# RWKV main part of a one-layer decoder trunk: packed operands, fewer transposes, a written order on four engines, and one filling block moved forward

## The chip, the cores and the metric

The kernel runs on one core of one Trainium2 chip. The core has five engines that run their own instruction streams in order: PE (matrix products and transposes, from a weight load and a moving operand), DVE (vector work), ACT (activations and copies), POOL (general vector work, and the issue of some DMAs) and SP (which here only issues DMAs). An instruction waits for semaphores that other engines or DMAs raise. The metric is the device time in microseconds of one execution: before, a median of 1507.03 us of 3 runs (1506.78 to 1507.43).

## What is computed

One layer of a hybrid decoder trunk, sequence 1024, model width 1024. Its mixing stage projects the normed input to 30 blocks of 128 columns and feeds three groups of heads:

```python
z = rmsnorm(h, norm_mix_g[l]) @ w_in[l]
a_q, a_f, a_i, a_g, b_q, b_k, b_v, c_in = jnp.split(z, splits, axis=-1)
o_a = hgrn2_mix(a_q, a_f, a_i, a_g, ...)          # 4 heads
o_b = dilated_window_mix(b_q, b_k, b_v)           # 4 heads, three dilations
o_c, v_first = rwkv7_mix(c_in, ...)               # 4 heads of 64
h = h + jnp.concatenate([o_a, o_b, o_c], axis=-1) @ w_out[l]
```

A gated convolutional feed-forward part and a gated per-layer embedding follow. The change is in `rwkv7_mix`, whose core is a recurrence over the sequence, one state matrix of 64 x 64 per head:

```python
def step(state, inp):
    r_t, w_t, k_t, v_t, kk_t, a_t = inp
    sa = jnp.einsum('bhvk,bhk->bhv', state, -kk_t)
    state = (state * w_t[:, :, None, :] + sa[..., None] * (kk_t * a_t)[:, :, None, :]
             + v_t[..., None] * k_t[:, :, None, :])
    return state, jnp.einsum('bhvk,bhk->bhv', state, r_t)
```

and whose result is normed per head (mean and variance over 64 values), gets a bonus term and a gate.

## The kernel before

**Projections.** One block of 128 output columns over the whole sequence is 8 K tiles times 2 halves of 512 columns, each as three products of split operands (high by high, low by high, high by low: L127, L129, L131), so 48 matmuls of 128x512. Input and weight are each split into a high and a low part (`xh`, `xl`, `whi`, `wlo`); the weight's low part is made on POOL or DVE in turn (`split_w`). `project_rest` makes such a block, finishes it (scaling on DVE, for some kinds a sigmoid on ACT, into `zst`, L440 to L447) and stores it by SP to a DRAM tile (L437), from which the HGRN and window stages load it later (`zload`, L475, into `zl`). These blocks are the filling: their products need nothing of RWKV's work.

**RWKV.** The four heads go in two pairs, one head on each half of the 128 partitions. For each pair `rwkv_prep` makes the decayed keys and the rest, `rwkv_inverse` inverts the triangular systems inside the chunks (`T` and `U` quads), then filling blocks follow, then `rwkv_main`, then more filling. The list `FILL = (6, 4, 4, 4)` says how many blocks are taken: one of the first six inside the preparation of pair one and five behind it, four around and behind its main part, one and three ahead of pair two's main part, four behind. The remaining four blocks of 22 are made in the HGRN stage by `project_late` (L449), in eight halves, tile name `zp`.

**The main part.** The sequence is 16 chunks of 64; `rwkv_group` does four chunks (u = 0 to 3) at a time, so four groups per pair. In a group:

- the removal keys (first half of `ar`), the keys `be` (bhat) and `kh` (khat) are copied into block-diagonal tiles `abd`, `bbd`, `kbd` (one 64x64 block per head), and each of the four chunks of each is transposed on PE (`pt`, L758, 4 transposes each); `v` is transposed directly (L762, 2 transposes). ACT copies the results to `xr`, `rb`, `kt`, `vt`
- `py` (L789, T by the spread scores AB), `sc` (L794, keys by `ar`), `pu` (L799, Y by U), `pk` (L804) build the operands
- `px` (L810) is U against `xr`, 192 columns a chunk: 128 of the block-diagonal removal keys, 64 values. `pgm` (L817) is X against `rb`, 256 columns a chunk: 128 for the output, 128 for the state, both block-diagonal, and DVE adds a block-diagonal `addend` (L818, GM)
- `pn` (L822, L823) is the state's own term; the state runs through the four chunks (`pS`, L836, then DVE, L837), and the output `pyo` takes three products a chunk (L838, L839, L841). ACT copies it to `y`, a tile of its own.

After the third group and after the third following block, `rwkv_norm` norms a half of `y`, transposes it (`yt`) and applies bonus and gate (`oc`).

**What sets the order.** A scheduler orders each engine's instructions by priorities and modelled times, except inside a `manual_schedule` block, where the engines named keep the order in which the code is written. In RWKV, before, only the preparation on PE stands in such a block; the main part is left to the scheduler, which puts single dense matmuls of the next filling block between the small ones and pulls one block of filling ahead of pair two's main part.

**The HGRN stage.** Two chains of HGRN heads (tiles `hsc`, `hpo`, `hk`, `qt`, `ho`), the window attention (`swq`, `swt`, `swo`) and the late halves F are interleaved by a written list (L322 to L325): at each odd round below 16 stands one F. A pair of HGRN heads ends with the normed output: sums `hss` on DVE, `hrs` on POOL (L998), `ho` on DVE (L1000), its transposes `vt` on PE (L1006) and a last DVE step into `zl` (L1007). The second pair of window heads is loaded by two DMAs that POOL issues (L475).

Of the kernel before, what the change touches and what calls it, by code (L numbers as in the profile page):

```python
# [10 lines left out]
F32 = mybir.dt.float32  # L11
# [3 lines left out]
ALU = mybir.AluOpType  # L15
# [3 lines left out]
P = 128  # L19
# [60 lines left out]
class Trunk:  # L80
# [11 lines left out]
    def load_w(self, src):  # L92
        nc = self.nc
        raw = self.wpool.tile([P, 1024], F32, tag="wraw", name=self.nm("wraw"), bufs=2)
        nc.sync.dma_start(raw, src)
        return self.split_w(raw)
# [12 lines left out]
    def split_w(self, raw):  # L109

        parts = []
        for b in (0, 1):
            self.uid += 1
            parts.append(self.split2(raw[:, b * HT:(b + 1) * HT], self.nc.gpsimd if self.uid % 2 else self.nc.vector))
# [190 lines left out]
    def phase_mix(self):  # L305
# [8 lines left out]
        with tc.tile_pool(name="hg", bufs=1) as slots, tc.tile_pool(name="sw", bufs=1) as sp:  # L314
# [8 lines left out]
            for r in range(36):  # L323
                order += "C" * (r in self.TURNS) + "A" + "B" * (r > 5) + "F" * (r % 2 and r < 16)
# [98 lines left out]
    def project_rest(self, js, hooks={}):  # L423


        nc = self.nc
        for j in js:
            ps = self.proj(j, hooks)
            t = self.keep.tile([P, T], F32, tag="zst", name=self.nm("zst"), bufs=2)
            kind = (j - 8) % 4 if j < 24 else 2  # L430
            parts = [(t, ps, self.R)]
            if j < 24 and kind < 3:
                parts = [(t[:, :HT], ps[:, HT:][:, ::-1], self.R[:, HT:][:, ::-1]), (t[:, HT:], ps[:, :HT], self.R[:, :HT])]
            for part in parts:
                self.finish(kind, *part)
            d = self.zpool.tile([P, T], F32, tag=f"z{j}", name=f"z{j}")
            nc.sync.dma_start(d, t)  # L437
            self.z[j] = d
# [50 lines left out]
    def rwkv(self):  # L489
# [7 lines left out]
        for p in (0, 1):  # L497
# [5 lines left out]
            self.project_rest([next(js) for _ in range(self.FILL[2 * p] - 1)])  # L503
            with tc.tile_pool(name=f"rk{p}", bufs=1) as rp:
                self.rwkv_main(p, rp, sg, d)
            for i in range(self.FILL[2 * p + 1]):
                self.project_rest([next(js)])
                if i == 2:
                    self.rwkv_norm(p, sg, d, 1)
        self.rest = list(js)  # L510

    FILL = (6, 4, 4, 4)

    def rwkv_prep(self, p, tp, lt, d, j):
# [51 lines left out]
        ar = self.slots.tile([P, 16, 2, 64], F32, tag="rk_ar", name=self.nm("ar"), bufs=1)  # L566
# [57 lines left out]
    def scores_open(self, d):  # L624
        for n in ("sc", "rb"):
            d[n] = self.slot(n).rearrange("p (c i) -> p c i", i=64)
# [47 lines left out]
    def rwkv_main(self, p, rp, sg, d):  # L674
        y = self.slot("y")
        y3 = y.rearrange("p (c v) -> p c v", v=64)
        S = None
        d.update(y=y, y3=y3)
        for g in range(4):
            S = self.rwkv_group(p, g, rp, d, y3, S)  # L680
            if g == 2:
                self.rwkv_norm(p, sg, d, 0)

    def rwkv_norm(self, p, sg, d, hf):

        nc, mxp, par = self.nc, self.mxp, self.par
        y, y3 = d["y"], d["y3"]
# [4 lines left out]
        sl, cs = slice(hf * HT, (hf + 1) * HT), slice(8 * hf, 8 * hf + 8)  # L692
        y, y3 = y[:, sl], y3[:, cs, :]
        if hf == 0:
            d["o"] = self.keep.tile([P, T], F32, tag="oc", name=self.nm("oc"), bufs=2)
        o = d["o"][:, sl]
        mean = self.spool.tile([P, 8], F32, tag="kr1", name=self.nm("gnm"), bufs=1)
        nc.vector.tensor_reduce(mean, y3, AX.X, ALU.add)
        nc.vector.tensor_scalar(mean, mean, 1.0 / 64, None, ALU.mult)
        nc.vector.tensor_tensor(y3, y3, mean.unsqueeze(2).broadcast_to([P, 8, 64]), ALU.subtract)  # L700
        nc.scalar.activation(o, y, AF.Square)
        var = self.spool.tile([P, 8], F32, tag="kr2", name=self.nm("gnv"), bufs=1)
        nc.vector.tensor_reduce(var, o.rearrange("p (c v) -> p c v", v=64), AX.X, ALU.add)
        nc.vector.tensor_scalar(var, var, 1.0 / 64, GN_EPS, ALU.mult, ALU.add)
        rs = self.spool.tile([P, 8], F32, tag="kr3", name=self.nm("gnr"), bufs=1)
        nc.gpsimd.tensor_tensor(rs, var, self.mhalf[:, :8], ALU.pow)
        nc.vector.tensor_tensor(y3, y3, rs.unsqueeze(2).broadcast_to([P, 8, 64]), ALU.mult)
# [16 lines left out]
    def rwkv_group(self, p, g, rp, d, y3, S):  # L724

        nc, mxp = self.nc, self.mxp
        cs = slice(4 * g, 4 * g + 4)
        ar, v, gC = d["ar"], d["v"], d["gC"]

        def c3(t):  # L730
            return t.rearrange("p (c i) -> p c i", i=64)[:, cs, :]
# [3 lines left out]

        ab = self.block_diag(rp, "abd", ar[:, cs, 0, :], nc.scalar)
        bb = self.block_diag(rp, "bbd", c3(d["be"]), nc.gpsimd)
        kb = self.block_diag(rp, "kbd", c3(d["kh"]), nc.gpsimd)
        if (rp, "add") not in self.bd:
            add = rt("addend", [P, 4, 2, 2, 64])  # L740
            nc.gpsimd.memset(add, 0.0)
            for u in range(4):
# [1010 lines left out]
```

## Time and profile before

| what | value |
|---|---|
| median of 3 runs | 1507.03 us (1506.78 to 1507.43) |
| the profiled execution, its own time | 1504.95 us |
| span of the profiled execution | 1503.2 us |
| busy PE, DVE, ACT, POOL | 1463.3, 1081.8, 635.7, 445.8 us |
| main part of pair one, of pair two (from the span's start) | 146 to 216 us, 350 to 417 us |
| HGRN and window stage | 443 to 660 us |
| PE busy in those three stretches | 67.8 of 70, 65.0 of 67, 201.5 of 217 us |

The span is the time from the first to the last instruction that the profile shows; the execution's own time is 1.75 us longer. The median is over other executions, so sums that come from the trace stand against 1504.95 and are carried over as differences. "Idle before" in a row is the time in which the engine stood still just ahead of the instruction, with the engine and line that ended it. A row of a timeline has the start in microseconds of the span, the duration, the engine, the line and the operation (output, then inputs), and how many records it holds. A matmul of fp32 operands shows as two records, one of the split operands as one. Matmuls overlap in the pipeline, so that the distance between two starts is shorter than the duration.

### The profile page before, as it was taken

Reading aid. Unit: us, or ns where it says so; the run is one execution under the profiler, and the core shown is the slowest. Engines: PE = TensorE matmul, PEld = TensorE weight load, DVE = VectorE, ACT = ScalarE, POOL = GpSimd, SP = SyncE. Lnnn points to the kernel's source line nnn. Section 1 sums busy time; section 2 is a strip of 40 time slices with the busy share of each in tenths; the row PEclk is TensorE's granted clock in tenths of the full one; section 3 lists DMA queues with packets and bytes.
Section 4 is the critical chain, followed back from the end, with each engine's and each line's share of the span. In section 5 each row is a group of like instructions: output and inputs, shape, how many; then the busy total and the mean of one; then the engine's idle time right before and its main releaser. Section 6 shows DMA issues by size and latency. Waiting matters only on the chain. (4 is left out here: it accounts for less than half of the span.)

```text
span 1503.2 us, 20149 instructions
## 1 busy us (share of the span) xinstructions
PE 1463.3 (97%) x7464; PEld 1212.3 (81%) x7464; DVE 1081.8 (72%) x1580; ACT 635.7 (42%) x1095; POOL 445.8 (30%) x367
## 2 busy tenths in 40 slices
PE   9999999999999989999999999999999999999996
PEld 7888887888877777778878888888888888888875
DVE  7666442775455667845798888888888889877685
ACT  6532422314323545524554444444444545455542
POOL 3234321315211123213234544444554000001342
PEclk9999999999999989999999999999999999999998
DMA  6124012133042122155333333333332893352343
GB/s 218 57 91 121 20 29 85 43 106 85 1 182 78 41 100 78 42 197 190 124 136 105 104 100 99 104 101 102 104 102 72 294 330 111 99 168 63 115 157 114
DMA packets 80019, 167.84 MB, mean 112 GB/s; under 512 B 20080, under 2 KB 22256, under 8 KB 79920
## 3 DMA queue, kind: packets, MB, share of 16 engines
q1 hardware_dynamic: 65568, 145.44, 29.9%
q10 hardware_dynamic: 13264, 17.04, 3.3%
q0 software_dynamic: 1088, 4.06, 0.8%
q8 instruction: 59, 0.97, 0.3%
q14 instruction: 40, 0.33, 0.1%
HBM read 120.12 MB, written 46.40 MB: 111 GB/s over the span
## 5 line engine op out<-in xcount | busy, mean ns | idle before, releaser
L127 PE MATMUL dp<-xh,whi 128*128 128x512 f32 x544 | 185.8, 400 | 1.0 <-ACT xh L371 1.0
L131 PE MATMUL dp<-xh,wlo 128*128 128x512 f32 x544 | 181.9, 392 | 1.3 <-POOL wlo L106 1.1
L129 PE MATMUL dp<-xl,whi 128*128 128x512 f32 x544 | 182.7, 393 | 0.4 <-DVE xl L372 0.3
L106 POOL TENSOR_TENSOR wlo<-raw,whi 128x512 fp32r<-128x512 f32 x84 | 138.0, 1662 | 77.8 <-ACT whi L104 77.8
L106 POOL TENSOR_TENSOR wlo<-wraw,whi 128x512 fp32r<-128x512 f32 x59 | 82.4, 1397 | 262.0 <-ACT whi L104 257.5
L104 ACT CAST whi<-wraw 128x512 fp32r<-128x512 f32 x120 | 73.2, 617 | 159.1 <-PE dp L129 119.6
L1225 PE MATMUL bg<-t,whi 128*128 128x512 f32 x352 | 132.7, 389 | 0.0
L127 PEld LDWEIGHTS dp<-xh,whi 128*128 128x128 f32 x544 | 100.8, 188 | 24.0 <-issue 3.3
L131 PEld LDWEIGHTS dp<-xh,wlo 128*128 128x128 f32 x544 | 101.8, 188 | 22.6 <-POOL wlo L106 1.5
L129 PEld LDWEIGHTS dp<-xl,whi 128*128 128x128 f32 x544 | 101.6, 188 | 22.0 <-DVE xl L372 1.2
L106 POOL TENSOR_TENSOR wlo<-s,whi 128x512 fp32r<-128x512 f32 x44 | 66.1, 1503 | 159.0 <-ACT whi L104 159.0
L1526 PE MATMUL bg<-t,whi 128*128 128x512 f32 x308 | 95.0, 389 | 0.0
L1526 PE MATMUL bv<-t,whi 128*128 128x512 f32 x308 | 94.8, 389 | 0.0
L104 ACT CAST whi<-raw 128x512 fp32r<-128x512 f32 x88 | 52.4, 619 | 97.4 <-PE bv L1225 48.9
L104 ACT CAST whi<-s 128x512 fp32r<-128x512 f32 x66 | 38.9, 620 | 120.1 <-PE bg L1225 113.0
L106 DVE TENSOR_TENSOR wlo<-wraw,whi 128x512 fp32r<-128x512 f32 x61 | 49.6, 813 | 43.6 <-ACT whi L104 40.9
L1225 PEld LDWEIGHTS bg<-t,whi 128*128 128x128 f32 x352 | 66.1, 188 | 13.7
L172 POOL TENSOR_TENSOR rst<-rst,mhalf 128x4 f32<-128x4 f32 (+1 forms) x9 | 10.2, 1132 | 221.7 <-DVE rst L170 221.7
L1526 PEld LDWEIGHTS bv<-t,whi 128*128 128x128 f32 x308 | 57.8, 188 | 12.0
L1526 PEld LDWEIGHTS bg<-t,whi 128*128 128x128 f32 x308 | 57.8, 188 | 11.9
L1225 PE MATMUL bg<-t,wlo 128*128 128x512 f32 x176 | 67.2, 389 | 0.0
L1522 ACT CAST t<-t 128x512 fp32r<-128x512 f32 x77 | 47.8, 622 | 45.7 <-PE bv L1526 29.9
(427 smaller groups left out, 3701.4 us busy)
## 6 DMA issues: line engine op xcount, KB each, us to landing
raw<-in_ffn_up_dram SPq DMA_DIRECT2D x44, 512.0 KB, 3.7
wraw<-in_w_in_dram SPq DMA_DIRECT2D x29, 512.0 KB, 3.8
z<-zst SPq DMA_DIRECT2D x18, 512.0 KB, 3.2
gb<-ct SPq DMA_DIRECT2D x33, 256.0 KB, 2.0
t<-gb SPq DMA_DIRECT2D x33, 256.0 KB, 2.8
t<-gt SPq DMA_DIRECT2D x33, 256.0 KB, 2.7
zl<-z SPq DMA_DIRECT2D x16, 512.0 KB, 3.5
wraw<-in_ple_gate_dram SPq DMA_DIRECT2D x16, 512.0 KB, 3.6
```

Source lines behind the costliest of these rows:

```text
L104: nc.scalar.copy(hi, src)
L106: eng.tensor_tensor(lo, src, hi.bitcast(F32), ALU.subtract)
L127: nc.tensor.matmul(ps[hf], wh, xh[hf], start=first, stop=False)
L129: nc.tensor.matmul(ps[hf], wh, xl[hf], start=False, stop=False)
L131: nc.tensor.matmul(ps[hf], wl, xh[hf], start=False, stop=last)
L172: nc.gpsimd.tensor_tensor(r2[:, :n], r[:, :n], self.mhalf[:, :n], ALU.pow)
L1225: nc.tensor.matmul(ps, w[part == 2][:, s], X[k][part == 1], start=start and k == part == 0, stop=k == 3 and part == 2, skip_group_check=no ...
L1522: nc.scalar.copy(xh, x)
L1526: nc.tensor.matmul(ps[m], wt[part == 2][:, m * P:(m + 1) * P], (xh, xl)[part == 1], start=k == part == 0, stop=k == NK - 1 and part == 2)
```

## The change

- **Half of the transposes.** `ar` is stored with its two halves apart, so that two chunks of one half are contiguous, and `ar`, `be`, `kh` are transposed as `v` was: two transposes of 128x128 hold four chunks of both heads. The results are put in their places by four copies of 64 partitions each (`place`), on ACT for `v`, `ar` and `kh`, on DVE for `be`. Only `kbd` stays block-diagonal.
- **Packed moving operands.** `px` moves 128 columns a chunk (64 packed keys, 64 values) and `pgm` 128 (`PB`: 64 for the output, 64 for the state). What used to come out block-diagonal is placed so by the copies into `X`, the additions into `GM` and copies on POOL into `RB`; the zeros around are written once per pair.
- **A written order.** The whole main part of a pair stands in a `manual_schedule` of PE, DVE, ACT and POOL. The filling inside is a generator (`project_steps`) of which each `fill(k)` takes k steps; a step is one K tile of one half, three dense matmuls. A group of pair one takes 11 steps, one of pair two 8. Finishing a block and splitting the next weight are put off to marked places (`pending`), and the splits go to POOL alone.
- **Result in the scores' place.** `y` takes the tile of the scores `sc`, which a group no longer needs when its output is written; the tile `y` is gone.
- **The norm in parts.** `rwkv_norm` becomes `rwkv_norm_in` (in up to four parts, between the steps of the third and fourth group) and `rwkv_norm_out`. The second half's output follows the last filling block.
- **Blocks.** `FILL` becomes (6, 4, 6, 3): five blocks ahead of pair two's main part, three in and behind it, 19 in all; three late blocks in place of four (`r < 14`).

The core of the diff:

```diff
-                order += "C" * (r in self.TURNS) + "A" + "B" * (r > 5) + "F" * (r % 2 and r < 16)
+                order += "C" * (r in self.TURNS) + "A" + "B" * (r > 5) + "F" * (r % 2 and r < 14)
...
+    def project_steps(self, js):
+        w = self.load_w(self.a["w_in"][js[0]])
+
+        def steps(w):
+            for n, j in enumerate(js):
+                ps = self.dps.tile([P, T], F32, tag="dp", name=self.nm("dp"))
+                raw = self.load_raw(self.a["w_in"][js[n + 1]]) if n + 1 < len(js) else None
+                nxt = []
+                self.pend["w"] = (lambda raw=raw, nxt=nxt: nxt.append(self.split_w(raw, self.nc.gpsimd))) if raw else None
+                for k in range(ND):
+                    if k == 6:
+                        self.pending("w")
+                    for hf in (0, 1):
+                        self.mm3({hf: ps[:, hf * HT:(hf + 1) * HT]}, w(k), self.X[k], k == 0, k == ND - 1, (hf,))
+                        if k == ND - 1 and hf:
+                            self.pend["z"] = lambda j=j, ps=ps: self.project_done(j, ps)
+                        yield n
+                w = nxt[0] if nxt else None
+        return steps(w)
...
-                self.rwkv_main(p, rp, sg, d)
-            for i in range(self.FILL[2 * p + 1]):
-                self.project_rest([next(js)])
-                if i == 2:
-                    self.rwkv_norm(p, sg, d, 1)
+                with tc.manual_schedule(engines={E.PE, E.DVE, E.Activation, E.Pool}):
+                    self.rwkv_main(p, rp, sg, d, steps)
+                    for _ in range(2):
+                        next(steps, None)
+                    self.pending("w")
+                    self.rwkv_norm_out(p, sg, d, 0)
+            self.rwkv_norm_in(p, d, 1)
+            for n in steps:
+                self.pending("z")
+            self.pending("z")
+            self.rwkv_norm_out(p, sg, d, 1)
         self.rest = list(js)
 
-    FILL = (6, 4, 4, 4)
+    FILL = (6, 4, 6, 3)
...
-        ar = self.slots.tile([P, 16, 2, 64], F32, tag="rk_ar", name=self.nm("ar"), bufs=1)
+        ar = self.slots.tile([P, 2, 16, 64], F32, tag="rk_ar", name=self.nm("ar"), bufs=1).rearrange("p a c i -> p c a i")
...
-        y = self.slot("y")
+        y = d["scf"]
...
+            pv = turn(lambda b: v[:, t2(b)])
+            fill(1)
+            Y = rt("Y", [P, 4, P])
+            py = mxp.tile([P, 4, P], F32, tag="mx", name=self.nm("py"))
...
+            nc.scalar.copy(Y, py)
+            if not last:
+                scores_bd(g + 1)
+            place(pv, Vt, 0, nc.scalar.copy)
+            place(turn(lambda b: ar[:, c2(b), 0, :].rearrange("p c i -> p (c i)")), Xr, 0, nc.scalar.copy)
...
+            fill(1)
+            U = t["U", g]
+            pu = mxp.tile([P, 4, P], F32, tag="mx", name=self.nm("pu"))
...
+            place(turn(lambda b: d["be"][:, t2(b)]), PB[:, :, 1, :], 0, nc.vector.tensor_copy)
...
+            place(turn(lambda b: d["kh"][:, t2(b)]), Kt, 64, nc.scalar.copy)
+            fill(1 + more)
...
+            fill(2)
+            px = mxp.tile([P, 4, P], F32, tag="mx", name=self.nm("px"))
+            for u in range(4):
+                nc.tensor.matmul(px[:, u, :], U[:, u, :], Xr[:, u, :], start=True, stop=True)
+            for q, copy in zip(Q, (nc.scalar.copy, nc.vector.tensor_copy)):
+                copy(X[q, :, q], px[q, :, 0:64])
+            nc.scalar.copy(X[:, :, 128:192], px[:, :, 64:128])
+            fill(2)
+            pg = mxp.tile([P, 4, 2, 64], F32, tag="mx", name=self.nm("pgm"))
+            for u in range(4):
+                nc.tensor.matmul(pg[:, u, :, :], X[:, u, 0:128], PB[:, u, :, :], start=True, stop=True)
...
+                if u == 0:
+                    fill(1)
```

On PE the change takes rows from 5283 to 5267; the transposes `pt` go from 112 to 64, the other small products keep their number.

More of the change, by code (lines that the diff above doesn't have):

```diff
@@ L698, in rwkv_norm @@
[L698 to L704, printed above, removed]
@@ L734, in rt @@
             return rp.tile(shape, F32, tag=name, name=self.nm(name), bufs=bufs)
[L736 to L742, printed above, removed]
-                nc.gpsimd.tensor_copy(add[:, u, 1, :, :], self.ident.rearrange("p (a b) -> p a b", b=64))
-            self.bd[(rp, "add")] = add
@@ L770, in rwkv_group, with fill @@
-        AK = rt("AKt", [P, 4, P])
-        RK = rt("RKt", [P, 4, P])
+        def fill(k):
+            for _ in range(k):
+                next(steps)
         def spread(dst, src, m, eng):
```

309 lines of the change are left out of this document (181 added, 128 removed).

## Prediction

> **What bounds the kernel now.** I read the page first: the span, the engines' busy shares and the clock by slices.
>
> ```profile
> span 1503.2 us, 20149 instructions
> ...
> PE 1463.3 (97%) x7464; PEld 1212.3 (81%) x7464; DVE 1081.8 (72%) x1580; ACT 635.7 (42%) x1095; POOL 445.8 (30%) x367
> ...
> PEclk9999999999999989999999999999999999999998
> ```
>
> PE is busy for 97% of the span, so the time is PE's. A change can save PE work, save the 40 us in which PE idles, or disturb the slices in which PEclk is 9. The second view is PE's groups of instructions over the first 700 us, different shapes apart. These are the four that the change touches (a record counts one pass; the mean is one record's pipelined duration):
>
> ```profile
> L817 PE MATMUL pgm<-rb,X 128*128 128x256 f32 x64 | 15.7, 387 | 0.3
> ...
> L810 PE MATMUL px<-xr,U 128*128 128x192 f32 x64 | 11.7, 326 | 0.0
> ...
> L789 PE MATMUL py<-T,ABt 128*128 128x128 f32 x64 | 9.1, 286 | 1.0 <-ACT xr L759 0.3 <-DVE T L782 0.3 <-DVE oc L715 0.3
> ...
> L758 PE MATMUL pt<-cst,kbd 128*128 128x128 f32 x32 | 4.8, 273 | 0.1
> ```
>
> The third view is PE's timeline of the first group of pair one. Columns are start, duration to the last end, line and operation; since records overlap, I price by the distance between starts.
>
> ```profile
> 146.31 0.60 PE L758 MATMUL pt<-cst,abd 128*128 128x128 f32 x4
> 146.74 0.60 PE L758 MATMUL pt<-cst,bbd 128*128 128x128 f32 x4
> ...
> 147.83 1.06 PE L789 MATMUL py<-T,ABt 128*128 128x128 f32 x8
> 148.73 1.06 PE L794 MATMUL sc<-ar,kbd 128*128 128x128 f32 x8
> ...
> 153.68 1.46 PE L810 MATMUL px<-xr,U 128*128 128x192 f32 x8
> 155.15 1.97 PE L817 MATMUL pgm<-rb,X 128*128 128x256 f32 x8
> 156.95 0.33 PE L822 MATMUL pn<-X,rb 128*128 128x64 f32 x2
> ...
> 159.35 0.39 PE L839 MATMUL pyo<-vt,RKt 128*128 128x64 f32 x2
> 159.55 0.48 PE L127 MATMUL dp<-xh,whi 128*128 128x512 f32 x1
> 159.87 0.39 PE L129 MATMUL dp<-xl,whi 128*128 128x512 f32 x1
> 160.10 0.33 PE L836 MATMUL pS<-S,GM 128*128 128x64 f32 x2
> ```
>
> Four transposes take 0.43 us (146.74 − 146.31). Eight records of 128 columns take 0.90 (148.73 − 147.83), eight of 192 take 1.47 (155.15 − 153.68) and eight of 256 take 1.80 (156.95 − 155.15). PE waits for nothing there: columns and transposes are what it pays for. The fourth view is the waits. In the window of the first main part, then in that of the second:
>
> ```profile
> PE pu L799 <- ACT Y L790: 1.4, 3, 0.8
> PE pk L804 <- DVE AKt L774: 0.4, 1, 0.4
> ```
>
> ```profile
> PE pu L799 <- ACT Y L790: 1.0, 2, 0.5
> PE py L789 <- ACT xr L759: 0.3, 2, 0.2
> PE py L789 <- DVE T L782: 0.3, 1, 0.3
> PE py L789 <- DVE oc L715: 0.3, 1, 0.3
> ```
>
> Together 1.4 + 0.4 + 1.0 + 0.3 + 0.3 + 0.3 = 3.7 us of PE idling. The rest of the RWKV part runs dense. The stage behind it does not; its two waits that matter here:
>
> ```profile
> PE vt L1006 <- DVE ho L1000: 4.7, 2, 3.0
> ...
> PE swq L1067 <- DVE zst L442: 2.3, 1, 2.3
> ```
>
> **The change part by part.** All sums are against the profiled execution, 1504.95 us (span 1503.2). It is 2.08 us below the median of 1507.03; I carry the difference in time over to the median.
>
> *Fewer transposes and columns.* Per group six transposes go (112 to 64 over eight groups): 48 × 0.43/4 = 5.2 us. pgm falls from 256 to 128 columns: 8 × (1.80 − 0.90) = 7.2 us. px falls from 192 to 128: by starts 8 × (1.47 − 0.90) = 4.6 us, by the groups' busy time 11.7 − 9.1 = 2.6; I take 3.5. All of it is on PE, which is the bound: −15.9. The Trainium skill, page "TensorE: Matmul & The Clock Gate", section "Back-to-back issue gap", states a sustained 81 ns per matmul at 128 columns and 131 ns at 512, so that columns would hardly count: with those figures, interpolated, an estimate of the same three terms is 48 × 0.081 + 64 × 0.017 + 64 × 0.008 = 5.5 us. The rows above (1.80 against 0.90) speak against that, and I sum by them.
>
> *The written order.* Before, the small matmuls of a group stood nearly together and the scheduler put dense ones between. Now a step of three dense matmuls (one K tile of a filling block for one half of its columns, L130 to L134) stands at fixed places. PE, start of pair one's first group, before (dp is a filling block):
>
> ```order
> L758 MATMUL pt_1266<-cst,abd_1242 128x128 x4
> L758 MATMUL pt_1272<-cst,bbd_1246 128x128 x4
> L758 MATMUL pt_1278<-cst,kbd_1250 128x128 x4
> L762 MATMUL pt_1284<-cst,v_692 128x128 x2
> L789 MATMUL py_1300<-T_1295,ABt_1291 128x128 x4
> L794 MATMUL sc_1307<-ar_483,kbd_1250 128x128 x4
> L127 MATMUL dp_1816<-xh_105,whi_1808 128x512
> L127 MATMUL dp_1816<-xh_89,whi_1808 128x512
> L799 MATMUL pu_1314<-U_1296,Y_1299 128x128 x4
> L804 MATMUL pk_1320<-vt_1265,AKt_1292 128x64 x4
> ```
>
> and after:
>
> ```order
> L816 MATMUL pt_1286<-cst,v_692 128x128 x2
> L130 MATMUL dp_1289<-xh_105,whi_1240 128x512
> L132 MATMUL dp_1289<-xl_106,whi_1240 128x512
> L134 MATMUL dp_1289<-xh_105,wlo_1242 128x512
> L856 MATMUL py_1296<-T_1259,ABt_1261 128x128 x4
> L816 MATMUL pt_1308<-cst,ar_483 128x128 x2
> L867 MATMUL sc_1315<-ar_483,kbd_1263 128x128 x4
> L130 MATMUL dp_1289<-xh_89,whi_1240 128x512
> L132 MATMUL dp_1289<-xl_90,whi_1240 128x512
> L134 MATMUL dp_1289<-xh_89,wlo_1242 128x512
> L877 MATMUL pu_1329<-U_1267,Y_1295 128x128 x4
> L816 MATMUL pt_1335<-cst,bhat_484 128x128 x2
> ```
>
> The block-diagonal transposes are gone; v, ar and bhat turn two at a time, and three dense matmuls stand in front of py and of pu. Each step has 3 × 0.23 = 0.68 us. The tightest wait is pu: it takes the scratch bank that v's transposes leave, so it needs Y and the four copies of Vt on ACT:
>
> ```profile
> 148.86 1.09 ACT L766 COPY vt<-pt 64x128 f32<-64x128 f32 x4
> 149.97 0.59 ACT L790 COPY Y<-py 128x512 f32<-128x512 f32 x1
> ```
>
> ACT needs 0.59 + 1.09 = 1.68 us after py. PE has two transposes 0.22, sc 0.81 and a step 0.68 = 1.71 in that time. It just fits. What does not fit, by the same walk: at each pair's start ACT still has the last block's output to do (about 0.5 us, twice), and pair two, with two steps less, waits for the state's second step (some 0.15 us in four groups). That is 1.6 in place of 3.7: −2.1. Bounds: −3.7 and, if each group waits 0.5 us more, +1.9.
>
> *Switching.* From a small to a dense matmul costs a little: in the timeline 159.55 to 159.87 is 0.32 against 0.23 for the next one, less 0.02 gained before it, so about 0.075 us an insertion. The order has 84 switches in the two main parts before and 116 after, 16 insertions more: +1.2.
>
> *Result in the scores' place, split copies, weight splits on GpSimd.* On DVE, ACT and POOL, which are busy 72, 42 and 30% of the span; covered by PE's steps as far as the walk above goes; 0. Uncovered they cost rival D's price.
>
> *One filling block moved forward.* 18 blocks become 19 in the RWKV part, and four late blocks become three, so halves seven and eight of zp leave the HGRN stage. One block is 48 matmuls × 0.23 (159.87 to 160.10) = 11.0 us of PE. The move is free only if the late stage shrinks by as much. PE there, before (ho is the output of a pair of HGRN heads, swt, hsc and swo belong to that stage):
>
> ```order
> L1090 MATMUL swt_4396<-cst,lg_4282 128x128 x4
> L923 MATMUL hsc_4412<-qt_3958,ks_4357 128x128 x4
> L127 MATMUL zp_4435<-xh_105,whi_4425 128x512
> L129 MATMUL zp_4435<-xl_106,whi_4425 128x512
> L131 MATMUL zp_4435<-xh_105,wlo_4427 128x512
> ...
> L131 MATMUL zp_4435<-xh_119,wlo_4431 128x512
> L1006 MATMUL vt_4464<-cst,ho_4329 128x128 x4
> L1006 MATMUL vt_4470<-cst,ho_4329 128x128 x4
> L923 MATMUL hsc_4480<-qt_3958,ks_4420 128x128 x4
> ```
>
> and after:
>
> ```order
> L1190 MATMUL swt_4461<-cst,lg_4353 128x128 x4
> L1190 MATMUL swt_4467<-cst,lg_4353 128x128 x4
> L1023 MATMUL hsc_4483<-qt_4027,ks_4428 128x128 x4
> L1106 MATMUL vt_4534<-cst,ho_4400 128x128 x4
> L1106 MATMUL vt_4540<-cst,ho_4400 128x128 x4
> L1023 MATMUL hsc_4554<-qt_4027,ks_4491 128x128 x4
> L1203 MATMUL swo_4565<-pT_4447,sV_3704 64x128
> ```
>
> Half seven was all that stood between hsc and vt of ho. The trace in that place, PE, then DVE:
>
> ```profile
> 529.16 0.80 PE L1067 MATMUL swq<-zl,zl 64*128 64x128 f32 x4 [2.55 <-DMA zl<-z]
> ...
> 541.83 0.47 PE L127 MATMUL zp<-xh,whi 128*128 128x512 f32 x1
> ...
> 547.40 1.03 PE L1006 MATMUL vt<-cst,ho 128*128 128x128 f32 x8
> ...
> 551.36 3.33 PE L1103 MATMUL swo<-pT,sV 128*64 128x128 f32 x32 [2.03 <-DVE zl L1007]
> ...
> 555.79 0.47 PE L127 MATMUL zp<-xh,whi 128*128 128x512 f32 x1
> ```
>
> ```profile
> 544.26 2.08 DVE L1000 TENSOR_TENSOR ho<-ho,hrs 128x1024 f32<-128x1024 f32 x1 [1.56 <-POOL hrs L998]
> ...
> 550.56 1.40 DVE L1007 SCALAR_TENSOR_TENSOR zl<-vt,par,zl 128x512 f32<-128x512 f32 x2
> ```
>
> The half covers 541.83 to 547.40 = 5.6 us. But ho ends on DVE at 544.26 + 2.08 = 546.3, and the steps behind it on DVE reach L1007 at 550.56, for which swo waits at 551.36. That chain does not have PE in it; only the scaling of zp (0.7 us) leaves it. So half seven gives back 0.7 us. Half eight, from 555.79 and equally long, has no such wait behind it: 5.6. And on POOL the pair of loads that ended at 529.16 in the timeline moves. Before (L475 DMA) and after (L502 DMA):
>
> ```order
> L926 TENSOR_TENSOR hk_3955<-hk_3955,zl_3904 128x2x256
> L926 TENSOR_TENSOR hk_3955<-hk_3955,hT_4000 128x2x64x4
> L926 TENSOR_TENSOR hk_3955<-hk_3955,hT_4000 128x2x16x16
> L106 TENSOR_TENSOR wlo_5563<-wraw_5555,whi_5561 128x512
> L475 DMA zl_4325<-z_3678 128x1024
> L475 DMA zl_4327<-z_3837 128x1024
> L998 TENSOR_TENSOR hrs_4409<-hss_4406,mhalf 128x8
> ```
>
> ```order
> L1026 TENSOR_TENSOR hk_4024<-hk_4024,zl_3973 128x2x256
> L1026 TENSOR_TENSOR hk_4024<-hk_4024,hT_4071 128x2x64x4
> L1026 TENSOR_TENSOR hk_4024<-hk_4024,hT_4071 128x2x16x16
> L157 TENSOR_TENSOR xl_4507<-oc_1640,xh_4506 128x512
> L108 TENSOR_TENSOR wlo_5630<-wraw_5622,whi_5628 128x512
> L157 TENSOR_TENSOR xl_4509<-oc_3267,xh_4508 128x512
> L502 DMA zl_4396<-z_3663 128x1024
> L502 DMA zl_4398<-z_3745 128x1024
> L1098 TENSOR_TENSOR hrs_4480<-hss_4477,mhalf 128x8
> ```
>
> xl, wlo, xl now stand ahead of both loads, where only wlo stood.
>
> ```profile
> 521.98 1.27 POOL L106 TENSOR_TENSOR wlo<-wraw,whi 128x512 fp32r<-128x512 f32 x1 [4.16 <-ACT whi L104]
> 523.19 1.11 POOL L475 DMA_DIRECT2D zl<-z  x2
> ...
> 557.45 1.69 POOL L154 TENSOR_TENSOR xl<-zl,xh 128x512 fp32r<-128x512 f32 x1 [8.43 <-ACT xh L152]
> ```
>
> Two splits of up to 1.7 us; part of this lies in POOL's idle time before wlo. Between 0 and 3.4 later, I take 2.7, all of it PE's wait for the loads (2.55 becomes 5.2). The late stage shrinks by 0.7 + 5.6 − 2.7 = 3.6: 11.0 − 3.6 = +7.4. Bounds: 0 and 11.0 + 2.7 = 13.7.
>
> *Entry of the stage.* The wait for zst (2.3 us above) goes, because the last block's output now stands ahead of HGRN's steps on DVE. The first loads stand behind that block's store on SP, so 0 to 2.3 comes back: −1.
>
> Sum: −15.9 − 2.1 + 1.2 + 7.4 − 1.0 = −10.4. Profiled 1494.6; median 1507.03 − 10.4 = **1496.6 us**.
>
> **The rivals.** *A: the late stage shrinks by the whole block.* For: PE is 97% busy, half eight has no wait behind it. Against: ho's chain. 0 instead of +7.4: −17.8, 1489.2 us.
>
> *B: it doesn't shrink.* DVE, not PE, paces that stage: L1007 and what follows. +13.7 instead of +7.4: −4.1, 1502.9 us.
>
> *D: the written order stalls.* In order on four engines, a late copy holds everything behind it. A group has twelve copies of 64 partitions more than before, at 1.09/4 = 0.27 us each, in rows where nothing can pass. At 10.4/8 = 1.3 us a group nothing is left: 1507. Against: two more steps (1.4 us of PE) lie between most of them and their readers.
>
> *C, slower: the clock.* After a gap PE runs at half speed: the same eight transposes took 1.03 us at 547.40 and here, after 2.96 us of waiting, 1.94; and over 520 to 540 the granted clock was 0.83.
>
> ```profile
> 586.71 1.94 PE L1006 MATMUL vt<-cst,ho 128*128 128x128 f32 x8 [2.96 <-DVE ho L1000]
> ```
>
> ```profile
> 520.00:540.00 20.00, 16.41 (x130) 13.24 (x129) 7.92 (x17) 11.25 (x21) 2.32 (x3) 0.83 0.46 164
> ```
>
> Without the halves there are gaps of about 5 us at 529 and 4 at 542, and a third at 551, with little dense work between. If PE never regains the clock from 529 to 584, the 55 us there, less 11 for the halves, 2 of waits and 7 already slow, are 35 us of work at half speed: up to +35, 1531.6. It decides from 10.4 us of such work. Against: 13 us lie between the first two gaps, and by the clock's row about 7 us at half speed ((1 − 0.83) × 20/0.5) follow a gap. The same page, section "Part 1: The HAM clock gate", gives about 3.4 us of idling to fall and as much of work to rise; by that an estimate of this rival is two gaps × 1.7 = 3.4 us. The trace agrees in kind, though a 2.96 us wait was already enough.
>
> That the change doesn't do what it says is out: the order shows the counts.
>
> **How the numbers follow.** Forecast 0.55, A 0.12, B 0.18, D 0.10, C 0.05. What a measurement can tell from no change is about 0.2%, 3.0 us. Faster: the forecast, A, three quarters of B, a little of D: 0.82. Same: the rest of B and half of D: 0.09. Slower: C and the rest of D: 0.09. The range leaves out C, the slower part of D and the far ends: 1487 (A with px at 4.6 and no idling) to 1505 (B and 0.25 us a group).
>
> **What would show it.** Right: pgm and px at 0.11 us a record; no wait of PE over 0.5 us in the main parts; 48 zp matmuls fewer; vt of ho waiting 4 us and swq of the loads 5. Wrong: waits of PE for ACT or DVE in every group (D); PEclk of 5 or 6 between 529 and 584 (C); PE idling in the late stage by the whole 11 us (B) or not at all (A).

## The result and the profile after

The changed kernel takes 1496.19 us (median of 4 runs, 1494.13 to 1498.82) where the kernel before takes 1506.9 (median of 4, 1506.31 to 1507.43; the 1507.03 of the forecast was a median of 3): a ratio of 0.993, 95% interval 0.9913 to 0.9947, or 10.7 us. The forecast was 1496.6. Of all executions used here, one of e8's six took 1611.66 us at a mean granted clock of 0.846, where e8's others show 0.989 to 0.993, and it is left out. The two profiled executions differ by 8.7 us (1504.95 and 1496.24), and it is this difference that the traces can divide up. First the page of the changed kernel:

```profile
span 1494.5 us, 20176 instructions
...
PE 1445.1 (97%) x7416; PEld 1199.0 (80%) x7416; DVE 1097.8 (73%) x1650; ACT 634.5 (42%) x1121; POOL 446.6 (30%) x362
...
PEclk9999999999999989999999999999999999999998
```

PE is 18 us less busy over a span that is 9 us shorter, so PE idles more than before: work went away, and waits came. The groups that changed, by form, with line numbers of the changed kernel:

```profile
L895 PE MATMUL px<-xr,U 128*128 128x128 f32 x64 | 8.4, 274 | 0.0
L902 PE MATMUL pgm<-pb,X 128*128 128x128 f32 x64 | 8.4, 274 | 0.0
...
L816 PE MATMUL pt<-cst,khat 128*128 128x128 f32 x16 | 3.5, 300 | 0.7 <-ACT xr L823 0.7
```

pgm fell from 15.7 to 8.4 us, px from 11.7 to 8.4; the four forms of transposes now have 16 records each. PE's timeline in the first group of pair one (start, duration, operation):

```profile
155.58 1.05 PE L895 MATMUL px<-xr,U 128*128 128x128 f32 x8
156.39 0.48 PE L130 MATMUL dp<-xh,whi 128*128 128x512 f32 x1
156.71 0.39 PE L132 MATMUL dp<-xl,whi 128*128 128x512 f32 x1
...
157.87 1.05 PE L902 MATMUL pgm<-pb,X 128*128 128x128 f32 x8
158.75 0.33 PE L914 MATMUL pn<-vt,kt 128*128 128x64 f32 x2
```

px takes 156.39 − 155.58 = 0.81 us and pgm 158.75 − 157.87 = 0.88 for eight records; they took 1.47 and 1.80. The two steps of three dense matmuls between them begin with 0.32 us (156.71 − 156.39), as nearly every step behind a small product does; a dense matmul behind another takes 0.23. PE's waits in the two main parts:

```profile
PE pt L816 <- ACT xr L823: 0.4, 1, 0.4
```

```profile
PE pS L932 <- DVE S L933: 0.6, 2, 0.5
PE pS L932 <- DVE S L928: 0.4, 1, 0.4
PE pt L816 <- ACT xr L823: 0.3, 1, 0.3
```

They add up to 1.7 us where there were 3.7. The stage behind is another matter:

```profile
PE vt L1106 <- DVE ho L1100: 8.0, 3, 4.4
PE swq L1167 <- DMA zl<-z: 5.3, 1, 5.3
PE hsc L1002 <- DVE hk L984: 3.7, 1, 3.7
```

To see where the time went, I take six places that both programs pass on PE, and compare when they do. The block moved forward (48 dense matmuls, 10.9 us) lies ahead of the second place.

| PE reaches | before | after | difference | gained or lost since the row above |
|---|---|---|---|---|
| first transpose of pair one's main part | 146.31 | 146.41 | +0.1 | |
| first transpose of pair two's main part | 349.94 | 349.29 | −0.6 | −0.7 with one more block |
| first vt of the HGRN stage | 443.46 | 433.75 | −9.7 | −9.1 |
| first head's transposes of values and keys | 510.44 | 503.54 | −6.9 | **+2.8** |
| last vt of ho | 657.52 | 644.95 | −12.6 | −5.7 with one block less |
| first product of the embedding | 755.00 | 743.48 | −11.5 | **+1.1** |
| end of the span | 1503.2 | 1494.5 | −8.7 | **+2.8** |

The fourth place is called the key transposes below; those of the keys themselves start 0.9 us later, in both kernels. RWKV gained 9.7 + 10.9 = 20.6 us, more than forecast; the rest of the program gave some of it back, at places that the forecast had wrong or did not have.

### The profile page after: what moved, and what is told of

It reads as the page before. It is cut to its first block, busy times and chain, and to the rows that moved or that the text cites. A ratio compares the mean times of both kernels' runs of the same rounds, so it can differ in the third digit from the quotient of the medians.

```text
span 1494.5 us, 20176 instructions
## 1 busy us (share of the span) xinstructions
PE 1445.1 (97%) x7416; PEld 1199.0 (80%) x7416; DVE 1097.8 (73%) x1650; ACT 634.5 (42%) x1121; POOL 446.6 (30%) x362
## 4 chain that ended last, share of the span: by engine, by line
PE 84%; DVE 6%; issue 4%; POOL 2%; DMA 2%; ACT 1%; DVEq 0%; POOLq 0%; ACTq 0%; SPq 0%
PE bg L1325 16%; PE bv L1325 12%; PE dp L130 8%; PE dp L134 8%; PE dp L132 8%; PE bg L1626 7%; PE bv L1626 7%; PE hsc L1023 2%; DMA zl<-z 1%; PE swq L1167 1%; PE swo L1203 1%; POOL wlo L108 1%; PE bv L130 1%; PE bv L132 1%; PE swt L1190 1%
## 5 line engine op out<-in xcount | busy, mean ns | idle before, releaser
L130 PE MATMUL dp<-xh,whi 128*128 128x512 f32 x560 | 202.7, 406 | 1.1 <-ACT xh L374 1.1
L134 PE MATMUL dp<-xh,wlo 128*128 128x512 f32 x560 | 194.4, 391 | 2.0 <-POOL wlo L108 1.1
L132 PE MATMUL dp<-xl,whi 128*128 128x512 f32 x560 | 194.5, 391 | 0.4 <-DVE xl L375 0.3
L108 POOL TENSOR_TENSOR wlo<-wraw,whi 128x512 fp32r<-128x512 f32 x64 | 88.0, 1379 | 233.2 <-ACT whi L106 203.9
L134 PEld LDWEIGHTS dp<-xh,wlo 128*128 128x128 f32 x560 | 105.0, 188 | 25.0 <-POOL wlo L108 1.5
L130 PEld LDWEIGHTS dp<-xh,whi 128*128 128x128 f32 x560 | 104.5, 188 | 23.6 <-issue 3.8
L132 PEld LDWEIGHTS dp<-xl,whi 128*128 128x128 f32 x560 | 105.2, 188 | 21.8 <-DVE xl L375 1.4
L1626 PEld LDWEIGHTS bg<-t,whi 128*128 128x128 f32 x308 | 57.7, 188 | 12.0
```

The lines of the kernel that those rows point to most:

```text
L108: eng.tensor_tensor(lo, src, hi.bitcast(F32), ALU.subtract)
L130: nc.tensor.matmul(ps[hf], wh, xh[hf], start=first, stop=False)
L132: nc.tensor.matmul(ps[hf], wh, xl[hf], start=False, stop=False)
L134: nc.tensor.matmul(ps[hf], wl, xh[hf], start=False, stop=last)
L1626: nc.tensor.matmul(ps[m], wt[part == 2][:, m * P:(m + 1) * P], (xh, xl)[part == 1], start=k == part == 0, stop=k == NK - 1 and part == 2)
```

## The experiments

Each kernel was timed beside the kernel before, in four to six executions, e4 in twelve. All ratios are against the kernel before. The diffs are cut to what matters; line numbers are those of each run's own kernel.

**e1: the block moved back.**

```diff
-    FILL = (6, 4, 6, 3)
+    FILL = (6, 4, 5, 3)
...
-... "F" * (r % 2 and r < 14)
+... "F" * (r % 2 and r < 16)
```

> The changed kernel with the block moved back: 18 blocks in the RWKV part (four ahead of pair two's main part), four late blocks in eight halves; all else as changed. Theory (from the two traces: the late stage shrank by 5.7 us where 11.1 us of products left it, so the move costs about 5.4 us): about 5 us faster than the changed kernel, 1491; if the order of DVE in the last stage, which in this build is that of the kernel before, was what cost the 2 to 4 us there, another 2 to 4, so 1487 to 1491. Rival A (the move was free): 1496, no difference. Rival B (the late stage could not shrink at all): 1485 or less. In the trace: vt of ho waits under 3 us again and swq for its loads about 2.5 us; the 3.7 us wait for hk at the stage's entry stays.

Measured: 1488.83 us (1486.08 to 1490.66), ratio 0.988 [0.9866, 0.9893]: 7.4 us faster than the changed kernel. The move was a loss. By places: RWKV becomes only 7.3 us shorter, not 10.9 (426.40 against 433.75 at the first vt). Of the missing 3.6 us, 2.6 are waits: pair two's main part, with one block less ahead of it, now waits more for ACT:

```profile
PE pk L890 <- ACT kt L823: 1.1, 2, 0.6
PE pt L816 <- ACT xr L823: 1.1, 2, 0.7
PE pu L877 <- ACT Y L857: 0.8, 1, 0.8
```

With those for pS, for an operation's issue and in pair one (0.3) the waits of both main parts are 4.3 us, not 1.7: the fifth block ahead of pair two did buy something. The other 1 us has no wait that the trace shows. In the HGRN stage its waits are those of the kernel before again (in the changed kernel 8.0 and 5.3):

```profile
PE vt L1106 <- DVE ho L1100: 4.8, 2, 3.0
...
PE swq L1167 <- DMA zl<-z: 2.2, 1, 2.2
```

and the last stages take 749.4 us from the embedding's first product, not 751.0.

**e2: the block moved forward in the kernel before.**

```diff
-    FILL = (6, 4, 4, 4)
+    FILL = (6, 4, 5, 4)
...
-... "F" * (r % 2 and r < 16)
+... "F" * (r % 2 and r < 14)
```

> The kernel before with the block moved forward alone: 19 blocks in the RWKV part, three late ones; nothing else changed. Theory: the move by itself costs about 5 us, so 1512; with the cost in the last stages that the changed kernel's trace shows (2 to 4 us) up to 1516. Rival A (free): 1507. Rival B (the late stage keeps its whole length): 1518. In the trace: vt of ho waits about 4 us.

Measured: 1512.41 us (1511.8 to 1513.31), ratio 1.0039 [1.0026, 1.0052], 5.7 us slower than before. So the move costs 5.7 us here and 7.4 in the changed kernel, about the size of the theory; but the place is another. From the key transposes to the last vt of ho the stage gives back 6.5 us of the block's 11 (140.6 against 147.1 us), much as in the changed kernel (5.7). But the entry, from the first vt to the key transposes, shrinks by another 3.8 us (63.2 against 67.0), where the changed kernel's grew by 2.8: here the wait at the entry went, as the forecast had said. So by the last vt of ho this kernel is only 1.2 us behind (658.75 against 657.52). The rest is lost behind it, 5.2 us of it from the embedding's first product on (753.4 against 748.2 us): a wait of PE that the kernel before does not have,

```profile
PE bv L164 <- DVE acc L198: 1.6, 1, 1.6
```

a wait for DVE's bv that is longer (2.8 us, not 1.6), and behind it a granted clock of 0.91 from 780 to 800, where the kernel before has 1.00.

**e3: no written order.**

```diff
-with tc.manual_schedule(engines={E.PE, E.DVE, E.Activation, E.Pool}):
+if True:
```

> The changed kernel without the written order of the main part: the scheduler orders PE, DVE, ACT and POOL there; packing, transposes, blocks as changed. Theory (the gain is in PE's removed work, the order only keeps waits at 1.7 us): 1 to 4 us slower than the changed kernel, 1497 to 1500, with waits of PE in the two main parts of 3 to 6 us in place of 1.7. Rival (the written order is what pays, the packing would drown in waits): 8 us or more slower, 1504 and up. Second rival (the scheduler does better with fewer switches): 1 to 2 us faster.

Measured: 1497.61 us (1496.89 to 1501.45), ratio 0.9947 [0.9933, 0.9961]: 1.4 us slower than the changed kernel by the medians, with intervals that overlap. The order is worth little, if anything. The waits in the main parts are 2.5 us, fewer than I had expected; dense matmuls cost 1.9 us more by their starts (85.4 against 83.5 us for 336), which fits the 22 more changes between small and dense in this order.

**e4: pgm with 256 columns again.**

```diff
...
-nc.tensor.matmul(pg[:, u, :, :], X[:, u, 0:128], PB[:, u, :, :], start=True, stop=True)
+nc.tensor.matmul(pg[:, u], X[:, 2 * hh + u, 0:128],
+                 PB[:, 2 * hh + u, :, :].unsqueeze(1).broadcast_to([P, 2, 2, 64]), start=True, stop=True)
...
```

> The changed kernel with pgm's moving operand widened again from 128 to 256 columns (the packed operand is read twice over, the second half of the result is not used), in two scratch banks of two chunks as before. Theory (columns are paid in full by PE: 64 records at 0.11 us more each): 7.2 us slower, 1503.4. Rival (a record of 256 columns costs hardly more than one of 128, as the sustained figures of a page would have it, 0.017 us each): 1 us slower, 1497.3. Second rival (PE has slack there): no difference.

Measured: 1503.95 us (1501.35 to 1509.37), ratio 0.9987 [0.9975, 0.9998]: 7.8 us slower than the changed kernel. RWKV alone is 6.6 us longer (440.42 − 146.46 against 433.75 − 146.41), and the timeline shows why:

```profile
157.91 1.89 PE L905 MATMUL pgm<-pb,X 128*128 128x256 f32 x8
159.64 0.33 PE L919 MATMUL pn<-vt,kt 128*128 128x64 f32 x2
```

Eight records of 256 columns take 159.64 − 157.91 = 1.73 us, against 0.88. The Trainium skill, page "TensorE: Matmul & The Clock Gate", section "Back-to-back issue gap", with its sustained 81 and 131 ns at 128 and 512 columns, would by an estimate have had about 1 us for this (64 records at 0.017 more each). For these fp32 products the measurement decides: from 128 columns on, columns are paid in full. Below that they are not. pk moves 64 columns a record, and its eight records take 154.11 − 153.30 = 0.81 us in the changed kernel, as much as px with 128:

```profile
153.30 1.00 PE L890 MATMUL pk<-vt,AKt 128*128 128x64 f32 x8
154.11 0.48 PE L130 MATMUL dp<-xh,whi 128*128 128x512 f32 x1
```

So packing these operands further than to 128 columns would not have paid in the same way.

**e5: the second norm earlier.**

```diff
-for n in steps:
+for i, n in enumerate(steps):
     self.pending("z")
+    if p and i == 9:
+        self.rwkv_norm_out(p, sg, d, 1)
 self.pending("z")
-self.rwkv_norm_out(p, sg, d, 1)
+if not p:
+    self.rwkv_norm_out(p, sg, d, 1)
```

> The changed kernel, with one thing moved: pair two's second norm and gate (the last readers of RWKV's tiles) stand ten steps into the rest of the last filling block in place of behind it. Theory (the first loads of the HGRN heads wait for RWKV's tiles to come free, 435.4 us in the changed kernel's trace, and have only half a late block to hide behind, hence 3.7 us of PE's waiting for hk and a half clock behind it): the loads start about 2.5 us earlier, the wait for hk falls to about 1 us, the stage's entry is 2 to 4 us shorter, 1492 to 1494. Rival (the loads wait for the filling block's own store and not for the tiles): no change at the entry, 1496. Second rival (the entry shrinks, but the scheduler's order in the last stages, which differs in this build, takes or gives as much): read by stage.

Measured: 1496.11 us (1494.81 to 1499.81), ratio 0.9923 [0.9909, 0.9937], no faster than the changed kernel. Read by stage, the gain at the entry is there: SP issues the first two loads of HGRN 3 us earlier. First the changed kernel's row of SP's queue, then this one's:

```profile
435.38 1.73 SPq L502 DMA_DIRECT2D zl<-z  x2
```

```profile
432.42 0.80 SPq L502 DMA_DIRECT2D zl<-z  x2
```

The stage's entry, first vt to key transposes, takes 501.12 − 434.14 = 67.0 us in place of 69.8. The wait for hk is gone; a new one of 2.0 us, for DVE's hS, takes part of its place. The median does not show the gain. In the profiled execution, the longest of the five (1499.81), the last stages took 756.6 us against 751.0, with granted clocks of 0.91 and 0.83 around waits there.

What held the loads? Here they stand ahead of the block's store on SP's queue and wait for the norm's step that reads the older tile (`oc`, L756, which ends at 432.27):

```profile
SPq L502 <- DVE oc L756: 12.4, 1, 12.4
```

So the tile alone can hold them, and moving the norm brings them forward. In the changed kernel the store left SP free at 435.22 and the same step ended at 435.32: there queue and tile came free together, and as the edit moved both, no run tells them apart. That the shorter entry pays in time is not settled either; see e8.

**e6: the late halves in other places.**

```diff
-... "F" * (r % 2 and r < 14)
+... "F" * (r in (1, 3, 5, 7, 11, 13, 15))
```

> The changed kernel with its six late halves in other rounds of the HGRN stage: the fifth is left out where it stood (ahead of the second pair's key transposes) and the last two stand two rounds later, so that one again stands between hsc and vt of ho. Theory (ho's chain through DVE and POOL lasts about 9 us whatever PE does, so a half put there costs nearly nothing and a half taken from a place without a wait gains its whole 5.6 us): 3 to 5 us faster than the changed kernel, 1491 to 1493, with vt of ho no longer waiting 4.4 us. Rival (the stage is bound by DVE from end to end; the wait only moves ahead to the loads or to hk): within 1 us, 1496.

Measured: 1485.86 us (1483.18 to 1489.35), ratio 0.9862 [0.9844, 0.9881]: 10.3 us faster than the changed kernel, over twice what I had expected; the profiled executions, whose traces are compared here, differ by 7.2 us. The waits of the stage:

```profile
PE vt L1106 <- DVE ho L1100: 3.6, 2, 1.8
...
PE swo L1203 <- DVE zl L1107: 3.2, 1, 3.2
PE hsc L1002 <- DVE hk L984: 2.5, 1, 2.5
...
PE swq L1167 <- DMA zl<-z: 0.4, 1, 0.4
```

vt of ho waits 3.6 us in place of 8.0, swq for its loads 0.4 in place of 5.3 and hk 2.5 in place of 3.7; swo waits anew (3.2). The half that was left out at its old place had covered no wait: the key transposes are reached 8.9 us sooner behind the first vt (60.9 us, not 69.8). And POOL issues the pair of loads 10 us earlier, since the splits of finished outputs, which follow the last late half, now stand behind them. POOL in the changed kernel, then here:

```profile
514.62 1.28 POOL L157 TENSOR_TENSOR xl<-oc,xh 128x512 fp32r<-128x512 f32 x1 [3.71 <-PE zp L134]
515.85 1.28 POOL L108 TENSOR_TENSOR wlo<-wraw,whi 128x512 fp32r<-128x512 f32 x1
517.08 1.29 POOL L157 TENSOR_TENSOR xl<-oc,xh 128x512 fp32r<-128x512 f32 x1
518.30 1.12 POOL L502 DMA_DIRECT2D zl<-z  x2
```

```profile
508.32 1.11 POOL L502 DMA_DIRECT2D zl<-z  x2 [4.76 <-PE swq L1167]
...
530.03 1.42 POOL L157 TENSOR_TENSOR xl<-oc,xh 128x512 fp32r<-128x512 f32 x1 [2.34 <-DVE qt L1028]
```


**e7: e1 and e5 together.** The edits are those of e1 and e5.

> The kernel of e1 (18 blocks in RWKV, four late ones) with the edit of e5. Theory: the two gains add, e1's 1488.8 less the 2 to 3 us of its wait for hk and its half clock: 1486 to 1487. Rival (e1's entry was already covered, what it waits for there is DVE's own queue): 1488.8. Second rival (the order in the last stages moves by as much the other way): up to 1491.

Measured: 1486.88 us (1484.39 to 1489.47), ratio 0.9866 [0.9849, 0.9883], 2.0 us below e1, with intervals that overlap. At the key transposes it is 0.3 us ahead of e1 (492.61 against 492.88): hk's wait of 2.5 us was replaced by one for zst of 1.6. The gain at the entry that e5 had does not add here; inconclusive.

**e8: e5 and e6 together.** The edits are those of e5 and e6.

> The changed kernel with the edits of e5 and e6 together: the second norm earlier, the six late halves in the rounds of e6. Theory (the two act at different places of the stage): e6's 1485.9 less up to 2.8 us of e5's shorter entry: 1483 to 1485. Rival (with the halves where they are in e6, the entry's wait for hk was already cheap, or the last stages take it back): 1486, no difference to e6.

Measured: 1483.89 us (median of five, 1483.29 to 1485.93), ratio 0.9848 [0.9834, 0.9862]: 12.3 us faster than the changed kernel and about 23 faster than the one before, the lowest median of all. The entry takes 57.7 us against e6's 60.9, and at the last vt of ho this kernel is 4.0 us ahead of e6 (631.28 against 635.32): the earlier norm shortens the entry here as in e5. But the medians of e6 and e8 are 2.0 us apart and their intervals overlap, so what it brings in time stays open.

**e9: four late blocks, put where the stage waits.**

```diff
-... "F" * (r % 2 and r < 16)
+... "F" * (r in (1, 3, 5, 7, 11, 13, 14, 19, 21))
```

The diff is against e7, whose blocks and earlier norm this kernel has.

> 18 blocks in RWKV and four late ones as in e1, the second norm earlier as in e7, and the eight late halves where the stage waits: the fifth is left out at its old place, one stands ahead of each of the first two waits of vt for ho and one ahead of swo, which waits for DVE's last step on ho. Theory (late halves cost PE only what they do not cover; the three waits are 3.0, 2.1 and 3.0 us in e1's trace): 3 to 6 us faster than e7, 1481 to 1484, and as fast as or faster than e8, since four blocks then cover more than three. Rival (DVE, which also scales the halves, paces the stage; waits only move on): 1486 to 1489.

Measured: 1489.7 us (1487.95 to 1490.08), ratio 0.9881 [0.9867, 0.9895]. It is 2.8 us above e7 by the medians, with intervals that overlap, and not the 3 to 6 us faster that I had expected: the theory fell. As the rival says, the waits only move on. From the first vt to the last vt of ho PE idles 12.7 us here and 12.8 in e7, and the whole takes 212.5 and 212.6 us; the time is 0.7 us above the rival's range. The halves stand in front of the waits, and the waits move onto them:

```profile
PE zp L130 <- DVE zl L1110: 2.7, 1, 2.7
PE vt L1109 <- ACT ob L1207: 2.4, 1, 2.4
```

The half put ahead of swo waits itself for the same DVE step that swo waited for, since it takes a scratch bank that this step reads; and vt of ho, behind the next half, now waits for ACT. Covering a wait needs work that does not itself wait for the engine that is late. That DVE paces the whole stage, the rival's reason, is not shown by this.

## Why the prediction was right

The time was right to 0.4 us, and much of that is luck. The mechanism was right in RWKV, but its gain was put 3.9 us too small (−16.8 forecast, −20.7 in the traces), and what the rest of the program takes back 5.6 us too small (+6.4 forecast, +12.0). The traces then add up to −8.7, where the medians differ by 10.7. By the prediction's own steps, from the distances between starts on PE, in us against the kernel before:

| step | forecast | traces |
|---|---|---|
| transposes | −5.2 | −6.7 |
| pgm | −7.2 | −7.3 |
| px | −3.5 | −5.2 |
| the written order: PE's waits | −2.1 | −1.9 |
| switching between small and dense | +1.2 | +1.8 |
| other small products | 0 | −1.4 |
| block moved forward: late stage | +7.4 | +5.2 to 5.4 |
| entry of the stage | −1.0 | +2.8 |
| last stages | 0 | +3.9 |
| sum | −10.4 | −8.7 |

*Removed work.* The mechanism was right, and e4 shows it by itself. I had sized px between two rows (2.6 and 4.6) and the price by starts was the nearer one; the busy times of these overlapping matmuls understate what a column costs. The transposes gave more than 48 × 0.11, since those of v cost 2.9 us for 16 in the kernel before and 1.1 now: py started up to 0.55 us behind the second of them, and the dense matmul that stands there now starts 0.03 us behind it.

*Written order.* Forecast 1.6 us of waits, found 1.7. The walk through ACT's copies was borne out where it was tightest: pu waits for nothing. The half microsecond that I gave to each pair's start is there too (0.4 and 0.3 us, in the first group of each): the last block's output stands on ACT ahead of the copies of the removal keys, for which the transposes of khat wait. The waits for the state's steps are 1.0 us (forecast 0.6). Rival D needed 1.3 us of waits in each of the eight groups; there are 1.7 us in all.

*The block.* The waits came as forecast: 4.4 us for ho (forecast 4) and 5.3 for the loads (5.2):

```profile
525.01 0.80 PE L1167 MATMUL swq<-zl,zl 64*128 64x128 f32 x4 [5.31 <-DMA zl<-z]
...
542.51 1.94 PE L1106 MATMUL vt<-cst,ho 128*128 128x128 f32 x8 [4.40 <-DVE ho L1100]
...
546.09 2.88 PE L1203 MATMUL swo<-pT,sV 128*64 128x128 f32 x32
...
549.89 1.04 PE L1150 MATMUL vt<-cst,zl 128*128 128x128 f32 x8
```

From the key transposes to vt of ho PE needs 39.0 us, 2.0 more than before, which agrees with half seven's 0.7 and the loads' 2.7. Half eight gave back more than its 5.6: from vt of ho to the next vt of the stage it is 549.89 − 542.51 = 7.4 us in place of 13.9, 6.6 less. The row of swo shows the reason: it has no wait, where it had one of 2.0 us for DVE's last step on ho. I had taken that step's place in DVE's queue as fixed. In the changed kernel it starts 1.3 us behind the end of ho, not 4.2:

```profile
540.30 2.07 DVE L1100 TENSOR_TENSOR ho<-ho,hrs 128x1024 f32<-128x1024 f32 x1 [1.56 <-POOL hrs L1098]
...
543.64 1.60 DVE L1107 SCALAR_TENSOR_TENSOR zl<-vt,par,zl 128x512 f32<-128x512 f32 x2
```

Of the steps that stood between the two before, the half's scaling (0.7 us) went with the half; the keys of the next head (L884 and L886, 0.8 and 1.2 us) and two steps of the window (L1074) now stand behind. Why the scheduler moved them no run shows; it did so in every kernel whose three late blocks stand as here (e2 to e5 too).

*The entry.* This is the step that failed: "The first loads stand behind that block's store on SP, so 0 to 2.3 comes back". The wait for zst went, but 3.7 us for hk came in its place, and the sixteen records behind it ran at half speed (3.41 us at 445.22, 1.95 for the same sixteen in the kernel before, at 455.00). The sentence named SP's queue. It left out the tiles that the loads are written to, which RWKV's second norm reads last; and that norm now stands behind the last filling block, where little is left to hide the loads. e5 moved only the norm, and the entry shrank by 2.8 us; in e2, where a block still follows the norm, there is no wait for hk at all and the entry is 63.2 us. Whether the queue alone would have held the loads as long in the changed kernel stays open, since it came free only 0.1 us ahead of the tile.

*The last stages.* I had put 0, and they take 3.9 us more. PE idles 2.8 us longer there: 1.6 in a wait for DVE's sums of squares, 0.9 in one for a weight's low part (0.2 before), and 0.4 in one for POOL. The other 1 us I can't place; the granted clock is 0.99 from the embedding on in both kernels.

```profile
PE bv L167 <- DVE acc L201: 1.6, 1, 1.6
...
PE dp L134 <- DVE wlo L108: 0.9, 1, 0.9
```

Nothing of the change is there; the order of DVE's instructions in these stages differs. The scheduler made it anew. The wait for acc, and that order of DVE, are in every trace with three late blocks (the changed kernel, e2, e3, e4, e5, e6, e8) and in none with four (before, e1, e7, e9), which share an order of their own. So the number of late blocks brings the wait; by which of the scheduler's choices stays open, as no run changed that order alone.

*The rivals.* A (the late stage shrinks by the whole block) and B (not at all) were both wrong by halves: behind its entry the stage gave back 5.7 of 11.1 us. And e6 shows that the answer depends on which half is left out, which neither rival asked. C did not come: the granted clock from 515 to 560 was 0.85, against 0.89 before. It recovered between the waits, as the 13 us between them had suggested: two matmuls of hpo take 0.63 us up to 531 and 0.39 from 531.5 on.

The verdict of the change as a whole: without the move it would have brought 17.9 us (e1 against the kernel before), and the block that was moved takes 7.4 of them back. Packing and fewer transposes make 19 us by the traces; the written order brings 1 to 2 at most, which the runs can hardly tell from nothing.

## What to carry to other kernels

On an engine that is busy for 97% of the time, removed columns and transposes were worth at least their distance between starts: for pgm 7.2 us by the rows before, 7.3 by the traces and 7.8 by e4's time. Before moving filling work out of a stage that waits, ask for each piece which wait it covers: taking out one half block shortened the stage by its 5.6 us and more, taking out another by almost nothing, and choosing the right one (e6) was worth 10 us, more than the written order. A stage's first loads can't start before the last reader of the memory they go to is done, so a last reader that is put behind the last filling block delays them.

## What the runs showed of the hardware

- A wait of PE shorter than the 3.4 us of idling that the Trainium skill gives for the clock to fall (page "TensorE: Matmul & The Clock Gate", section "Part 1: The HAM clock gate") can be followed by half speed. In the changed kernel eight transposes behind a wait of 1.81 us took 1.94 us (granted clock 0.50 from 576 to 578 us); behind one of 1.77 us, at the end of the stage, they took 1.06 (granted clock 1.00 from 644 to 648). The section calls the window in which activity is watched free-running, so that its place could decide between the two; no run here shows the window itself, nor why so short a wait was enough.

```profile
575.33 1.94 PE L1106 MATMUL vt<-cst,ho 128*128 128x128 f32 x8 [1.81 <-DVE ho L1100]
```

```profile
644.95 1.06 PE L1106 MATMUL vt<-cst,ho 128*128 128x128 f32 x8 [1.77 <-DVE ho L1100]
```

- The same wait varies between builds in which nothing differs at that place. In the changed kernel, e3 and e6 DVE's instructions behind the last vt of ho stand in the same order; from product tp7 to product tp4 of the feed-forward part PE takes 6.2 us in the first two and 7.3 in the third. PE's wait for DVE's bv there is 1.6 us in the first two and 2.7 in the third, where the granted clock was 0.91 from 760 to 780. Executions of one kernel differ likewise (1494.13 to 1498.82 for the changed one, at mean granted clocks of 0.989 and 0.985), so that differences of 2 us, as between e1 and e7 or e6 and e8, are not settled by four or five executions.
